# Combination and w_oa operations in halves, and row and square additions on GpSimd

## The chip, the cores and the metric

The kernel runs on one core of one Trainium2 chip. The metric is the device time of one execution in microseconds; the time of a kernel is the median of several runs. Before the change it is 2155.13 us, the median of 3 runs that lie between 2155.13 and 2161.53. The profile shows another execution, which took 2158.47 us; its span from the first to the last instruction is 2156.7 us, at a mean granted TensorE clock of 0.995.

## The reference

One layer of a decoder trunk, all in f32, over 1024 prompt tokens and 32 sample tokens that share the weights (cut to what is computed):

```python
def swiglu(x, w1, w3, w2):
    return (jax.nn.silu(x @ w1) * (x @ w3)) @ w2

def combine_groups(outs, lses):
    w = jax.nn.softmax(jnp.stack(lses, axis=-1), axis=-1)
    o = jnp.sum(jnp.stack(outs, axis=-2) * w[..., None], axis=-2)
    return o.reshape(*o.shape[:-2], ATT_OUT_W)

def trunk_layer(x, ...):
    h = layer_norm(ALPHA * x + 0.5 * swiglu(x, f1_w1, f1_w3, f1_w2), ln1_g, ln1_b)
    z = h @ w_in + b_in
    ...
    for g, (window, dil) in enumerate(ATT_GROUPS):     # 3 dilated attention groups, 4 heads each
        ...
    att = combine_groups(outs, lses)                   # 256 columns
    yb, vrows = sgu_branch(uv, sgu_ln_g, sgu_ln_b, sgu_ws, sgu_b)   # 512 columns
    mix = (jax.nn.sigmoid(ga) * (att @ w_oa) + jax.nn.sigmoid(gb) * (yb @ w_ob)) @ w_out
    h = layer_norm(ALPHA * h + mix, ln2_g, ln2_b)
    h = layer_norm(ALPHA * h + 0.5 * swiglu(h, f2_w1, f2_w3, f2_w2), ln3_g, ln3_b)
    return h, new_bufs, vrows
```

The model width is 1024, the inner width of each FFN 2816.

## The kernel before

**Tiles.** Activations lie transposed: features on the 128 partitions, tokens along the free axis. The 1056 tokens (NT; the 1024 of the prompt are NP) form 4 chunks (NC) of 264 (C). The residual stream is eight rows of 128 features (KB = 8), held for each chunk as two tiles `Y[c][j]` of 128 x (4 x 264); "rows" below means these blocks of 128 features.

**Products.** A product in f32 is made from values split in a high and a low part. `split` (L251) casts on ScalarE (ACT, L252) and subtracts on VectorE (DVE, L253); `mm3` (L237) issues three matmuls for each tile of weights, all on L241. Results gather in PSUM: three banks of tag `mm` take turns for the blocks, five of tag `ax` serve the rest. A bank is free for the next block when its eviction has read it.

**Stages.** First FFN (its large products by schemes with seven products in place of eight; its last weights, the output stage, in plain blocks), LN1, the projection w_in with attention and the gated branch beside it, then the combination of the attention groups, the products with w_ob and w_oa, w_out, LN2, the second FFN and LN3.

**The output stage of an FFN.** For each chunk c and each row n, `block(n, c)` issues 12 matmuls and the eviction L924, which adds the product to the row. Beside it run, step by step, the generators that `tick` advances from three queues (bg, slow, mid):

- `gather` (L525) adds the rows of a chunk, two by two, into a tile of 128 x 528 (L532). Its first additions are made in the last steps of the seven-product scheme, the last by `center`.
- `center` (L536) folds the two halves (L544), adds the share of the plain weights (L545), forms the mean over the features with a matmul of ones (L548) and subtracts it from the rows (L554).
- `square_step` (L572) squares a row on ScalarE (L593) and adds the squares of each pair of rows to those of the chunk (L597), 128 x 528.
- `norm` (L599) folds the squares (L603), forms the variance with three small matmuls (L606), takes the reciprocal root (L654 to L659 or L663 to L667), spreads it by matmuls (L620) and multiplies (L631).

w_out (`mix`, eviction L1707, 24 matmuls a block) uses the same helpers for LN2.

**GpSimd.** It (POOL) combines weights for the seven-product schemes (`prep`, L385 to L393) and makes small casts of one column (`held`, L109), each of which takes a buffer in its turn once the buffer is free.

**Combination and w_oa.** `combine(hp)` (L1321) works out the weights of the three groups for a pair of heads, writes them to memory (`cD`, L1354), loads them back over 64 partitions each (L1350), multiplies each group's output by them (L1361) and adds the groups (L1363). `sample_join` (L1444) does the same for the sample tokens (L1452 to L1470, with a transposition on TensorE at L1467). In `mix` (L1564) `split_att` (L1568) splits the combined outputs, `product` (L1575) multiplies a product in PSUM into a gate (L1581), `local(n)` does so for w_ob, and the loop from L1676 for w_oa: after the four chunks of row n the two gated branches are added (L1688) and the sum is split for w_out (L1690).

**The order.** Operations go to the engines in an order made before the run: a scheduler takes the program as it is written, with a model of the durations, and keeps each engine's instructions in the order it finds. What stands under `urgent` (the evictions among it) goes ahead of what is not; fences and `issue_after` fix some pairs. Each engine then works its list off in order, and an instruction that waits holds up what stands behind it.

Of the kernel before, what the change touches and what calls it, by code (L numbers as in the profile page):

```python
# [16 lines left out]
ALU = mybir.AluOpType  # L17
# [6 lines left out]
KB = D // P  # L24
NP = 1024
NS = 32
NT = NP + NS
C = 264
NC = NT // C
# [53 lines left out]
class Trunk:  # L83
# [441 lines left out]
    def gather(self, c, i, m):  # L525

        y = self.Y[c]
        new = y[i // 2][:, 2 * (i % 2) : 2 * (i % 2) + 2]
        if i == 1:
            m = self.M([P, 2, C])  # L530
        if i:
            self.nc.vector.tensor_tensor(m, y[0][:, :2] if i == 1 else m, new, op=ALU.add)  # L532
        return m

    def center(self, c, hs, rest, m=None, parts=1):
# [36 lines left out]
    def square_step(self, c, n, tail=False):  # L572

        nc = self.nc
        tt = nc.vector.tensor_tensor
        y = self.Y[c][n // KH][:, n % KH]
        if n % 2 == 0 or tail:
            self.sq = self.M([P, 2, C])
        sq = self.sq
        if tail:  # L580
            s = self.sqs[c]
            if n == KB - 2:
                with self.urgent():
                    nc.scalar.activation(sq[:, 0], y, AF.Square)
                tt(s[:, 0], s[:, 0], s[:, 1], op=ALU.add)
                tt(s[:, 0], s[:, 0], sq[:, 0], op=ALU.add)
            else:
                with self.urgent():
                    tt(sq[:, 0], y, y, op=ALU.mult)
                    tt(s[:, 0], s[:, 0], sq[:, 0], op=ALU.add)  # L590
            return
        with self.urgent():
            nc.scalar.activation(sq[:, n % 2], y, AF.Square)  # L593
        if n == 1:
            self.sqs[c] = sq
        elif n % 2:
            tt(self.sqs[c], self.sqs[c], sq, op=ALU.add)  # L597

    def norm(self, c, i, mode, Y, s):  # L599
        nc = self.nc  # L600
# [720 lines left out]
    def combine(self, hp):  # L1321
        nc = self.nc
        raw = self.raw.pop(hp)
        t = [raw[:, g] for g in range(3)]
        nat = lambda g, x: x.rearrange("p (r b) -> p b r", r=GROUPS[g][1])
        row = lambda g, x: x.rearrange("p (b r) -> p b r", r=GROUPS[g][1])
        mn = self.X([16, P], "cmin", 1)
        for g in (1, 2):
            x = mn if g == 2 else t[0][:, 0]
            nc.vector.tensor_tensor(row(g, mn), row(g, x), nat(g, t[g][:, 0]), op=ALU.min)  # L1330
        for g in range(3):
            x = nat(g, t[g][:, 0])
            nc.vector.tensor_tensor(x, row(g, mn), x, op=ALU.subtract)
        nc.scalar.activation(raw[:, :, 0], raw[:, :, 0], AF.Exp)
        nc.vector.tensor_tensor(raw[:, :, 1], raw[:, :, 1], raw[:, :, 0], op=ALU.mult)
        for g in (1, 2):
            x = mn if g == 2 else t[0][:, 1]
            nc.vector.tensor_tensor(row(g, mn), row(g, x), nat(g, t[g][:, 1]), op=ALU.add)
        nc.vector.reciprocal(mn, mn)
        for g in range(3):  # L1340
            nc.vector.tensor_tensor(row(g, t[g][:, 1]), row(g, mn), nat(g, t[g][:, 0]), op=ALU.mult)
        yield
        att = self.att[hp]
        cbs = deque()

        def load(g):
            if g < 3:
                cb = self.held([P, NP])
                for h in range(2):
                    nc.sync.dma_start(cb[64 * h : 64 * h + 64], self.cD[hp, g, h].partition_broadcast(64))  # L1350
                cbs.append(cb)

        for g in range(3):
            nc.sync.dma_start(self.cD[hp, g].rearrange("h (a x) -> (h a) x", a=8), t[g][:, 1])  # L1354
        load(0)
        load(1)
        yield from self.pause(3)
        for g in range(3):
            aT = self.attT.pop((hp, g))
            load(g + 2)  # L1360
            nc.vector.tensor_tensor(aT, aT, cbs.popleft(), op=ALU.mult)  # L1361
            if g:
                nc.vector.tensor_tensor(att[:, :NP], att[:, :NP], aT, op=ALU.add)  # L1363
            yield

    def sample_rows(self, *blocks):
# [197 lines left out]
    def mix(self):  # L1564
        nc, a = self.nc, self.a
        att, mt = [], [None] * KB

        def split_att():  # L1568
            for hp in range(2):
                h, l = self.S([P, NT], F32R), self.S([P, NT], F32R)  # L1570
                for o in (slice(0, NP), slice(NP, NT)):
                    self.split(h[:, o], l[:, o], self.att[hp][:, o])
                att.append((h, l))

# [95 lines left out]
        ta = [self.fetch_z(26 + n) for n in range(3)]  # L1670
# [4 lines left out]
        m2 = []  # L1675
        for n in range(KB):  # L1676
# [3 lines left out]
            if n + 3 < KB:  # L1680
                m = NLEAD + NTAIL - KB + n + 3
# [3 lines left out]
            for c in range(NC):  # L1685
                product(wa, att, c, ta[n])
                self.tick(0, 1)
            nc.vector.tensor_tensor(mt[n], mt[n], ta[n], op=ALU.add)  # L1688
            m2.append((self.S([P, NT], F32R), self.S([P, NT], F32R)))
            self.split(*m2[n], mt[n])  # L1690
            done += 1
            if EARLY + n < KB:
                local(EARLY + n)
# [211 lines left out]
```

## Time and profile before

| | |
|---|---|
| median of 3 runs | 2155.13 us (2155.13 to 2161.53) |
| the profiled execution | 2158.47 us |
| its span | 2156.7 us |
| instructions | 43261 |
| mean granted TensorE clock | 0.995 |
| DVE, ACT, GpSimd busy in the span | 1552.1, 889.5, 323.5 us |

How to read it: engines are PE (TensorE's matmuls), PEld (its weight loads), DVE, ACT, POOL (GpSimd) and SP (SyncE, which issues DMAs). A group of instructions stands as line, engine, operation, result <- operands, count, then busy time and the mean duration in ns; a row of the timeline as start in the span, duration, engine, line, operation, and in square brackets the idle time just before with what ended it. The names of tiles carry the pool: S, W, R, Q, M and X lie in SBUF, mm and ax in PSUM; W, R and Q hold weights, M intermediate results, X small ones. The page has the span in 40 slices of 53.9 us:

```profile
PE   9999999999999999999999999999999999999997
DVE  8876767747789834887766758787667767657887
POOL 0432322200000012223000000000323333100000
PEclk9999999999999999999999999999999999999998
```

A digit is the busy share of the slice in tenths, for PEclk the granted clock in tenths of full speed. GpSimd has work in the two FFNs' weights and in the middle of w_in, and nearly none in the stages where the rows are added and squared.

### The profile page before, as it was taken

To read this page: it belongs to the slowest core of one execution; us is meant where nothing else is said; L and a number is where in the kernel's file an instruction comes from. 1 tells how busy PE (TensorE), PEld (TensorE's weight loads), DVE (VectorE), ACT (ScalarE), POOL (GpSimd) and SP (SyncE) were. 2 spreads that over 40 slices of the span, in tenths; PEclk is the share of its full clock that TensorE was granted. 3 is DMA by queue.
4 is the path that set the end of the run, shared out by engine and by line. 5 is a ranking of instruction groups with operands and counts; after the bars stand their busy time and mean duration, and the time that the engine had idled before them with its cause. 6 is when DMAs were issued, how large, how long until landed. Compare 5 with 4: busy or idle time off the path is not lost.

```text
span 2156.7 us, 43261 instructions
## 1 busy us (share of the span) xinstructions
PE 2124.5 (99%) x17307; PEld 2086.6 (97%) x17307; DVE 1552.1 (72%) x2727; ACT 889.5 (41%) x1680; POOL 323.5 (15%) x249
## 2 busy tenths in 40 slices
PE   9999999999999999999999999999999999999997
PEld 8999999999999999999988889999999999999997
DVE  8876767747789834887766758787667767657887
ACT  5444444422124644334375544264444444421224
POOL 0432322200000012223000000000323333100000
PEclk9999999999999999999999999999999999999998
DMA  4444545598884335676865755423454544596852
GB/s 154 146 139 170 184 164 169 190 345 311 326 327 167 130 113 174 196 237 207 281 220 164 230 176 189 154 100 119 140 178 149 190 165 159 194 408 267 310 185 81
DMA packets 168378, 426.51 MB, mean 198 GB/s; under 512 B 24353, under 2 KB 59793, under 8 KB 165489
## 3 DMA queue, kind: packets, MB, share of 16 engines
q1 hardware_dynamic: 167744, 423.21, 56.4%
q8 instruction: 135, 2.21, 0.4%
q10 hardware_dynamic: 432, 0.54, 0.1%
q14 instruction: 67, 0.54, 0.1%
HBM read 304.31 MB, written 165.57 MB: 218 GB/s over the span
## 4 chain that ended last, share of the span: by engine, by line
PE 85%; DVE 5%; DMA 5%; issue 1%; POOL 1%; ACT 1%; SPq 1%; ACTq 0%; DVEq 0%; POOLq 0%
PE ax L241 44%; PE mm L241 37%; DMA M<-kv 2%; PE ax L1205 1%; DVE W L253 1%; PE ax L1252 1%; DMA R<-wz 1%; PE ax L1229 1%; DVE M L1428 1%; DMA S<-zD 1%; DMA S<-cD 1%; DVE X L1433 0%; DVE S L631 0%; DMA S<-hD 0%; PE ax L620 0%
## 5 line engine op out<-in xcount | busy, mean ns | idle before, releaser
L241 PE MATMUL mm<-S,W 128*128 128x264 f32 x5400 | 715.7, 287 | 7.9 <-ACT S L252 2.6
L241 PE MATMUL ax<-S,W 128*128 128x264 f32 x5400 | 706.7, 284 | 0.7 <-ACT S L1033 0.5
L241 PEld LDWEIGHTS mm<-S,W 128*128 128x128 f32 x5400 | 677.6, 189 | 21.6 <-issue 8.5
L241 PEld LDWEIGHTS ax<-S,W 128*128 128x128 f32 x5400 | 676.3, 188 | 3.5 <-ACT S L1033 1.7
L241 PE MATMUL ax<-S,S 128*128 128x264 f32 x3240 | 475.7, 284 | 1.8 <-ACT S L1033 1.7
L241 PEld LDWEIGHTS ax<-S,S 128*128 128x128 f32 x3240 | 427.7, 188 | 2.4 <-ACT S L1033 1.9
L241 PE MATMUL mm<-S,S 128*128 128x264 f32 x2280 | 359.6, 286 | 2.7 <-DVE S L924 2.7
L241 PEld LDWEIGHTS mm<-S,S 128*128 128x128 f32 x2280 | 311.3, 189 | 4.1 <-ACT M L593 2.2
L252 ACT CAST W<-R 128x256 fp32r<-128x256 f32 (+2 forms) x175 | 130.7, 764 | 309.3 <-PE mm L241 140.1
L385 POOL TENSOR_TENSOR Q<-R 128x512 f32<-128x512 f32 x49 | 69.9, 1428 | 797.7 <-DMA R<-w13b 219.9
L253 DVE TENSOR_TENSOR W<-R,W 128x256 fp32r<-128x256 f32 (+2 forms) x175 | 156.8, 899 | 22.4 <-ACT W L252 21.4
L252 ACT CAST W<-Q 128x1024 fp32r<-128x1024 f32 (+1 forms) x78 | 76.8, 984 | 218.6 <-POOL Q L386 88.0
L819 DVE SCALAR_TENSOR_TENSOR S<-ax,S 128x264 f32<-128x264 f32 x240 | 99.3, 427 | 66.8 <-PE ax L241 66.4
L461 DVE TENSOR_TENSOR S<-ax,M 128x264 f32<-128x264 f32 x82 | 32.6, 432 | 148.7 <-PE ax L241 148.7
L253 DVE TENSOR_TENSOR S<-Q,S 128x1024 fp32r<-128x1024 f32 (+1 forms) x78 | 111.3, 1427 | 5.5 <-ACT S L252 5.4
L109 POOL CAST S<-ones 128x1 fp32r<-128x1 f32 x36 | 13.6, 384 | 676.0 <-PE ax L241 414.0
L253 DVE TENSOR_TENSOR W<-Q,W 128x1024 fp32r<-128x1024 f32 (+1 forms) x78 | 90.3, 1158 | 29.0 <-ACT W L252 28.9
L252 ACT CAST S<-Q 128x1024 fp32r<-128x1024 f32 (+1 forms) x78 | 76.7, 984 | 67.8 <-PE ax L241 47.2
L253 DVE TENSOR_TENSOR S<-S,M 128x528 fp32r<-128x528 f32 x72 | 83.9, 1165 | 3.7 <-ACT M L252 2.4
L386 POOL TENSOR_TENSOR Q<-Q,R 128x512 f32<-128x512 f32 x49 | 82.7, 1688 | 2.7
L252 ACT CAST S<-R 128x512 fp32r<-128x512 f32 (+1 forms) x62 | 41.9, 676 | 94.2 <-DMA sumsA<-S 39.6
L393 POOL TENSOR_TENSOR Q<-R,Q 128x512 f32<-128x512 f32 x49 | 80.2, 1637 | 1.2
(209 smaller groups left out, 2051.1 us busy)
## 6 DMA issues: line engine op xcount, KB each, us to landing
ws<-st SPq DMA_DIRECT2D x144, 256.0 KB
S<-sumsA SPq DMA_DIRECT2D x63, 528.0 KB
S<-sumsB SPq DMA_DIRECT2D x63, 528.0 KB
M<-kv SPq DMA_DIRECT2D x96, 256.0 KB
sumsA<-M SPq DMA_DIRECT2D x90, 264.0 KB
sumsB<-M SPq DMA_DIRECT2D x90, 264.0 KB
R<-w13b SPq DMA_DIRECT2D x44, 512.0 KB
R<-w13a SPq DMA_DIRECT2D x42, 512.0 KB
```

What stands on the lines that cost most here:

```text
L241: mm = lambda a, b, s, e: nc.tensor.matmul(o, a[:, cc], b, start=s, stop=e, skip_group_check=True)
L252: a = self.nc.scalar.copy(hi, src)
L253: b = self.nc.vector.tensor_tensor(lo, src, hi.bitcast(F32), op=ALU.subtract)
L385: tt(s12[:, lo], cd[:, lo], cd[:, hi], op=ALU.add)
L386: tt(s12[:, hi], s12[:, lo], ab[:, lo], op=ALU.subtract)
L393: tt(s34[:, hi], ab[:, hi], s12[:, hi], op=ALU.subtract)
L461: go(one, 5, False, lambda x: tt(h[:, x, 1], one[x], p7[:, x], op=ALU.add))
L819: nc.vector.scalar_tensor_tensor(y(x, r, e), bank[x], HALF, y(x, r, e), op0=ALU.mult, op1=ALU.add)
L1205: nc.tensor.matmul(pS[h][:, r, :nk], q[e, i * P : (i + 1) * P], k[e, k0 : k0 + nk], start=True, stop=True)
L1229: nc.tensor.transpose(pT[r][:, h, o], s[:, r, h, o], self.ident)
L1252: nc.tensor.matmul(pv[0][e, (i % 4) * P : (i % 4 + 1) * P], V[:, i - (nb - 1) + b, e], sT[:, r, h, b * P : b * P + P], start=b == 0, stop= ...
L1428: nc.vector.tensor_tensor(t, t, p.unsqueeze(1).to_broadcast(t.shape), op=ALU.mult)
```

## The change

Four edits. (1) `gather`: the additions of rows 1 and 2 of a chunk's three (i = 1, 2) go to GpSimd; the last (i = 3) stays on DVE. (2) `square_step`: the additions of squares go to GpSimd, except those of the last chunk. (3) `combine`: each multiplication and addition of 128 x 1024 becomes two of 128 x 512. (4) `split_att` splits its prompt tokens in two halves of 512, and the w_oa loop adds and splits the gated branches in two halves of 528. No matmul and no DMA is added or removed.

```diff
@@ gather
         if i:
-            self.nc.vector.tensor_tensor(m, y[0][:, :2] if i == 1 else m, new, op=ALU.add)
+            engine = self.nc.gpsimd if i < KB // 2 - 1 else self.nc.vector
+            engine.tensor_tensor(m, y[0][:, :2] if i == 1 else m, new, op=ALU.add)
         return m
@@ square_step
         elif n % 2:
-            tt(self.sqs[c], self.sqs[c], sq, op=ALU.add)
+            (tt if c == NC - 1 else nc.gpsimd.tensor_tensor)(self.sqs[c], self.sqs[c], sq, op=ALU.add)
@@ combine
-            nc.vector.tensor_tensor(aT, aT, cbs.popleft(), op=ALU.mult)
-            if g:
-                nc.vector.tensor_tensor(att[:, :NP], att[:, :NP], aT, op=ALU.add)
+            cb = cbs.popleft()
+            for o in (slice(0, 512), slice(512, NP)):
+                nc.vector.tensor_tensor(aT[:, o], aT[:, o], cb[:, o], op=ALU.mult)
+            for o in (slice(0, 512), slice(512, NP)) if g else ():
+                nc.vector.tensor_tensor(att[:, o], att[:, o], aT[:, o], op=ALU.add)
             yield
@@ mix, split_att
-                for o in (slice(0, NP), slice(NP, NT)):
+                for o in (slice(0, 512), slice(512, NP), slice(NP, NT)):
                     self.split(h[:, o], l[:, o], self.att[hp][:, o])
@@ mix, w_oa loop
-            nc.vector.tensor_tensor(mt[n], mt[n], ta[n], op=ALU.add)
             m2.append((self.S([P, NT], F32R), self.S([P, NT], F32R)))
-            self.split(*m2[n], mt[n])
+            for o in (slice(0, NT // 2), slice(NT // 2, NT)):
+                nc.vector.tensor_tensor(mt[n][:, o], mt[n][:, o], ta[n][:, o], op=ALU.add)
+                self.split(*(x[:, o] for x in m2[n]), mt[n][:, o])
```

The scheduler reorders what stands around these operations. In the whole program GpSimd's list goes from 254 instructions to 305: 17 additions each come to it in the first FFN's output stage, in w_out and in the second FFN's output stage, 8 of rows and 9 of squares. In the first FFN the square additions stand behind all casts L109 of chunk 2.

DVE in the first FFN's output stage, from the eviction (L924, after the change L925) of the third block of chunk 0 to that of the fourth; L554 (L555) subtracts the mean from rows, L253 splits a weight, L532 (L533) adds rows. Before:

```order
L924 SCALAR_TENSOR_TENSOR S_5361<-mm_7973,S_5361 128x264
L554 TENSOR_TENSOR S_5361<-S_5361,ax_7971 128x528
L253 TENSOR_TENSOR S_7995<-R_7993,S_7994 128x1024
L532 TENSOR_TENSOR M_7678<-M_7678,S_5582 128x528
L554 TENSOR_TENSOR S_5361<-S_5361,ax_7971 128x528
L554 TENSOR_TENSOR S_5554<-S_5554,ax_7971 128x528 x2
L253 TENSOR_TENSOR S_8283<-R_8281,S_8282 128x1024
L924 SCALAR_TENSOR_TENSOR S_5361<-mm_8000,S_5361 128x264
```

After:

```order
L925 SCALAR_TENSOR_TENSOR S_5361<-mm_7973,S_5361 128x264
L533 TENSOR_TENSOR M_7678<-M_7678,S_5582 128x528
L555 TENSOR_TENSOR S_5361<-S_5361,ax_7971 128x528 x2
L555 TENSOR_TENSOR S_5554<-S_5554,ax_7971 128x528
L253 TENSOR_TENSOR S_7995<-R_7993,S_7994 128x1024
L555 TENSOR_TENSOR S_5554<-S_5554,ax_7971 128x528
L925 SCALAR_TENSOR_TENSOR S_5361<-mm_8000,S_5361 128x264
```

One weight split of 128 x 1024 has left this stretch, and the row addition stands ahead of the four subtractions.

DVE in the combination of the second pair of heads: L1361 (after the change L1364) multiplies by the weights loaded from `cD`, L1363 (L1366) adds the groups, L1581 (L1584) are evictions of w_ob's products, L1461 and L1464 belong to `sample_join`. The tile mm_15522 of before is mm_15532 after. Before:

```order
L1581 TENSOR_TENSOR S_15104<-S_15104,mm_15522 128x264
L1461 SCALAR_TENSOR_TENSOR X_15497<-M_15392,X_15489,X_15497 128x64
L1361 TENSOR_TENSOR S_15061<-S_15061,S_15298 128x1024
L1461 SCALAR_TENSOR_TENSOR X_15497<-M_15392,X_15489,X_15497 128x64
L1581 TENSOR_TENSOR S_15104<-S_15104,mm_15536 128x264
L1361 TENSOR_TENSOR S_14348<-S_14348,S_15302 128x1024
L1464 COPY X_15497<-X_15497 128x64
L1581 TENSOR_TENSOR S_15104<-S_15104,mm_15550 128x264
L1363 TENSOR_TENSOR S_15061<-S_15061,S_14348 128x1024
```

After:

```order
L1584 TENSOR_TENSOR S_15107<-S_15107,mm_15512 128x264
L253 TENSOR_TENSOR W_15527<-R_15526,W_15527 128x512
L1364 TENSOR_TENSOR S_15066<-S_15066,S_15303 128x512 x2
L1584 TENSOR_TENSOR S_15109<-S_15109,mm_15532 128x264
L1364 TENSOR_TENSOR S_14348<-S_14348,S_15307 128x512 x2
L1584 TENSOR_TENSOR S_15109<-S_15109,mm_15546 128x264
L1366 TENSOR_TENSOR S_15066<-S_15066,S_14348 128x512
L1584 TENSOR_TENSOR S_15109<-S_15109,mm_15560 128x264
```

The first multiplication now stands ahead of the eviction of mm_15532, and the operations of `sample_join` have gone behind; the rows between hold two halves at a time.

TensorE near the end of the program: three matmuls L606 (L607) form chunk 2's variance among the blocks of chunk 3. Before:

```order
L241 MATMUL mm_25754<-S_25072,S_25191 128x264
L606 MATMUL ax_25670<-ones,M_25513 128x1 x3
L241 MATMUL mm_25754<-S_25073,S_25191 128x264
L241 MATMUL mm_25754<-S_25072,S_25192 128x264
L241 MATMUL mm_25770<-S_24994,S_25233 128x264
```

After:

```order
L241 MATMUL mm_25808<-S_25032,S_25271 128x264
L241 MATMUL mm_25808<-S_25033,S_25271 128x264
L241 MATMUL mm_25808<-S_25032,S_25272 128x264
L607 MATMUL ax_25708<-ones,M_25551 128x1 x3
L241 MATMUL mm_25808<-S_25062,S_25271 128x264
```

The variance stood two matmuls before the end of a block; now it stands three matmuls into the next.

## Prediction

> **What bounds the kernel now.** The page first: its span, its busy shares, then the chain that ended last.
>
> ```profile
> span 2156.7 us, 43261 instructions
> PE 2124.5 (99%) x17307; PEld 2086.6 (97%) x17307; DVE 1552.1 (72%) x2727; ACT 889.5 (41%) x1680; POOL 323.5 (15%) x249
> PE 85%; DVE 5%; DMA 5%; issue 1%; POOL 1%; ACT 1%; SPq 1%; ACTq 0%; DVEq 0%; POOLq 0%
> ```
>
> TensorE is busy in all but 32 us, and the change leaves its 17,307 matmuls as they are. So an edit can only win what TensorE waits for, or lose by adding waits. Where are those waits? The view by stretches, cut at the places where the change moves instructions, tells it. Columns: us of the stretch; busy us (and instructions) of PE, weight load, DVE, ACT, POOL; granted clock; DMA share; GB/s.
>
> ```profile
> 655.00:672.00 17.00, 14.99 (x109) 14.74 (x109) 15.40 (x28) 6.94 (x12) 0.00 (x0) 0.90 0.70 236
> 672.00:700.00 28.00, 27.14 (x219) 26.66 (x218) 26.32 (x47) 16.33 (x32) 0.00 (x0) 1.00 0.28 97
> 1262.00:1303.00 41.00, 37.08 (x302) 35.79 (x303) 33.02 (x78) 16.03 (x21) 0.00 (x0) 1.00 0.55 161
> 1303.00:1357.00 54.00, 53.27 (x427) 52.05 (x425) 46.34 (x75) 21.78 (x28) 1.24 (x2) 1.00 0.60 198
> 1390.00:1452.00 62.00, 62.00 (x511) 61.81 (x510) 49.25 (x81) 32.31 (x62) 1.69 (x6) 1.00 0.20 70
> 2090.00:2120.00 30.00, 30.00 (x244) 29.74 (x243) 25.88 (x52) 10.27 (x23) 0.00 (x0) 1.00 0.00 1
> 2120.00:2145.00 25.00, 22.41 (x182) 21.93 (x181) 18.01 (x45) 12.09 (x29) 0.00 (x0) 0.99 0.22 88
> ```
>
> The output stage of the first FFN (655 to 700) loses 2.9 us, the combination (1262 to 1303) 3.9, w_oa 0.7, w_out (1390 to 1452) nothing, the second FFN's output stage nothing up to 2120, and its tail 2.6. DVE is 93% busy from 655 to 700 (41.72 of 45 us), far above its mean of 72%: there it co-bounds.
>
> **The first FFN's output stage, first wait.** TensorE's timeline:
>
> ```profile
> 660.87 3.09 PE L241 MATMUL mm<-S,S 128*128 128x264 f32 x24
> 665.97 4.70 PE L241 MATMUL mm<-S,S 128*128 128x264 f32 x24 [2.00 <-DVE S L924]
> 676.57 1.73 PE L241 MATMUL mm<-S,W 128*128 128x264 f32 x12 [0.62 <-DVE S L924]
> 680.54 4.65 PE L241 MATMUL mm<-S,S 128*128 128x264 f32 x36 [0.23 <-DVE S L924]
> ```
>
> Three banks take turns; a block of 12 matmuls lasts about 1.5 us, and the next needs the bank that L924 has still to empty. At 663.9 the fourth eviction is late by 2.00 us, and the 24 matmuls behind it take 4.70 us where the 24 before took 3.09: another 1.61. The stretches say why: one that held the wait, and the next.
>
> ```profile
> 663.25:666.67 3.42, 1.42 (x12) 1.23 (x12) 3.40 (x7) 2.32 (x5) 0.00 (x0) 1.00 0.60 216
> 666.67:670.08 3.41, 3.41 (x18) 3.41 (x17) 3.41 (x7) 1.69 (x5) 0.00 (x0) 0.50 0.79 265
> 1284.40:1287.80 3.40, 2.00 (x17) 1.81 (x16) 2.21 (x4) 0.62 (x1) 0.00 (x0) 1.00 1.05 201
> ```
>
> After a stretch with TensorE 42% busy the granted clock is 0.50 for 3.41 us; the stretch at 1284.4, 59% busy, has no such follower. I read the limit as lying between. The Trainium skill, "TensorE: Matmul & The Clock Gate", What's actually happening, gives the half-rate state after at least one idle window of about 3.4 us. The trace disagrees: 2.00 us of waiting did it. By the page the 1.61 us would not depend on this wait and would stay, and the sum would end at 2156.3.
>
> The built order drops one weight split (L253) and keeps the rest between the third and the fourth eviction:
>
> ```profile
> L253 DVE TENSOR_TENSOR S<-R,S x4: 1215/1222/1227, 656.7 to 667.4; 128x1024 fp32r<-128x1024 f32 x4
> L924 DVE SCALAR_TENSOR_TENSOR S<-mm,S x64: 399/425/434, 656.2 to 2141.5; 128x264 f32<-128x264 f32 x64
> L597 DVE TENSOR_TENSOR M<-M,M x35: 694/700/710, 668.9 to 2139.5; 128x528 f32<-128x528 f32 x35
> ```
>
> That is 1.22 us earlier; the matmul of the mean stands four matmuls later (0.5 us), and the remaining row addition, which fills that gap, covers about half of it. I take 1.0 us off the wait. Then 1.0 us stays, the stretch is 71% busy, the clock holds, and the 1.61 us go too: **-2.6 us**. Bounds: 0 (order without effect) to -3.6 (wait gone).
>
> **The same stage, later waits.** Now 0.62 + 0.23 = 0.85 us. In the new order the evictions of mm_8153 and mm_8180 have a split (1.2), two subtractions L555 (2.4 together) and L545 (0.4) between them, 4.0 us against the 2.9 us that two blocks give: a wait of 1.1. Between mm_8079 and mm_8105 stand 3.2 us: 0.3. The price of GpSimd comes on top. No row has a 128x528 addition on it; nearest is 128x512:
>
> ```profile
> L391 POOL TENSOR_TENSOR Q<-R,R 128x512 f32<-128x512 f32 x49 | 75.8, 1547 | 14.7 <-ACT M L457 11.0 <-DVE S L253 3.7
> L489 DVE TENSOR_TENSOR M<-S x18: 699/1735/1750, 78.0 to 1866.1; 128x528 f32<-128x528 f32 x18
> ```
>
> So an addition takes about 1.6 us there instead of 0.70. And it does not run beside DVE for free: L489 at 128x528, two SBUF operands, takes 1735 ns at the median in stretches where GpSimd adds, where L597 of the same shape takes 700. A DVE operation with two SBUF operands that meets a GpSimd addition pays up to 1.04 us; L924, with one operand from PSUM, keeps 399 to 434 ns throughout. Nine square additions leave DVE here (9 x 0.70 = 6.3 us), and if about half of them collide, some 4.5 us come back. The total is covered by DVE's freed time; what counts is a collision just ahead of an eviction, and I price that at 0.35. New waits 1.1 + 0.3 + 0.35 = 1.75 against 0.85: **+0.9 us**, bounds -0.85 and +6 (every collision of chunks 0 and 1 lands in front of an eviction, 6 x 1.04).
>
> **GpSimd's own queue.** It already holds the buffer casts L109, in order, and the square sums stand behind those of chunk 2. They are no hindrance as long as their buffers are free before the first sum:
>
> ```profile
> 654.07 0.42 POOL L109 CAST S<-ones 128x1 fp32r<-128x1 f32 x1 [1.28 <-PE ax L241]
> 709.21 1.12 POOL L109 CAST S<-ones 128x1 fp32r<-128x1 f32 x1 [54.73 <-PE mm L241]
> ```
>
> The last cast ahead of the sums ran at 654.07, the first sum at 668.9 (L597's first row above); the next casts come after the sums. Cost 0; without that cover chunk 0's norm would wait.
>
> **Combination in halves.** DVE and TensorE around it:
>
> ```profile
> 1284.68 1.23 DVE L1361 TENSOR_TENSOR S<-S,S 128x1024 f32<-128x1024 f32 x1 [3.20 <-DMA S<-cD]
> 1286.59 1.70 PE L241 MATMUL mm<-S,W 128*128 128x264 f32 x12 [1.40 <-DVE S L1581]
> 1287.35 1.23 DVE L1361 TENSOR_TENSOR S<-S,S 128x1024 f32<-128x1024 f32 x1 [0.91 <-DMA S<-cD]
> 1288.83 0.30 PE L1467 MATMUL ax<-ident,X 128*128 128x128 f32 x1 [0.54 <-DVE X L1464]
> 1292.91 1.74 PE L241 MATMUL mm<-S,W 128*128 128x264 f32 x12 [0.65 <-DVE S L1581]
> 1295.44 6.09 PE L241 MATMUL mm<-S,W 128*128 128x264 f32 x48 [0.79 <-DVE S L253]
> ```
>
> The multiplication waits for a DMA (3.20 us idle), not for the operation's length, and the evictions L1581 queue behind it on DVE; TensorE waits 1.40 + 0.54 + 0.65 + 0.79 = 3.38 us. Halves shorten none of the DMA. In the new order the first multiplication stands one eviction earlier relative to the blocks: mm_15532 is emptied after it, where its counterpart mm_15522 was emptied before. So TensorE runs out of banks one block (1.45 us) earlier, about 2.5 us of waiting instead of 1.40. Then 1.2 instead of 0.65, as mm_15546 waits for the second load; the 0.54 goes, since the transposition moves behind the w_ob blocks, and 0.4 is left of the last: 4.1 against 3.38, **+0.7 us**. Bounds -1.7 (half of the waits go) and +3.
>
> **w_oa in halves.** The two waits at its end:
>
> ```profile
> 1337.80 19.03 PE L241 MATMUL mm<-S,W 128*128 128x264 f32 x150 [0.46 <-DVE S L1581]
> 1356.73 0.43 DVE L1707 SCALAR_TENSOR_TENSOR S<-mm,S 128x264 f32<-128x264 f32 x1 [2.88 <-DMA S<-hD]
> ```
>
> At 1356.7 DVE waits for a load, which halves do not touch. An early half helps the first: **-0.2 us**, bounds -0.8 and +0.3 (eight extra additions and splits, on a DVE with 7.7 us to spare).
>
> **w_out and the second FFN's output.** TensorE loses nothing there now, with a DVE that is 79% and 86% busy; 17 and 17 additions leave it. **0**, bounds 0 and +3.
>
> **The tail.**
>
> ```profile
> 2143.07 0.81 PE L620 MATMUL ax<-ident,X 128*128 128x128 f32 x6 [1.66 <-DVE X L659]
> 2147.22 1.42 PE L620 MATMUL ax<-ident,X 128*128 128x128 f32 x6 [2.68 <-DVE X L667]
> ```
>
> Chunk 2's variance matmul moves five matmuls towards the end (5 x 0.12 = 0.6 us), its chain on DVE ends one small operation later (0.2), and chunk 3's variance stands behind it on TensorE: **+0.8 us**, bounds 0 and +1.3.
>
> Sum: -2.6 + 0.9 + 0.7 - 0.2 + 0.8 = -0.4 us. The profiled execution took 2158.47 us (span 2156.7 and 1.8 around it), and would take 2158.1; the median of the runs shown is 2155.13, so **2154.7 us**.
>
> **Rivals.** *Relief*: DVE, freed of additions, is never late in 655 to 700 (2.00 + 1.61 + 0.85 = 4.5 us), half of the combination's waits go (1.7) and w_oa's 0.8: 7.0 us, 2148.1. For it: each of the three waits ends on L924 behind a DVE that is 93% busy. Against: the median of 1735 ns, and a combination that waits for a DMA. *Contention* (the other side): additions on GpSimd hold up DVE's splits ahead of evictions. Price 6.2 us for chunks 0 and 1, the first gain of 2.6 gone, 0.7 and 0.8 as above, and 1 us in the second FFN: 8.7 us, 2163.8. It decides once the collisions ahead of one eviction exceed the 2.9 us lead of two banks; against it stands that six additions are spread over 20 us. The Trainium skill, "SBUF — State Buffer", Who interferes with whom, has it as a lock: of a DVE instruction with two SBUF inputs and a GpSimd one that reads SBUF, the second blocks until the first is done. The trace agrees (1735 against 700 ns). *Clock*: the 2.5 us of waiting in the combination leave a stretch under half busy; forecast plus 1.6 and 0.4, 2156.7; the 59% now are the only row for the limit.
>
> **How the numbers follow.** Forecast 0.42, clock 0.11, relief 0.25, contention 0.22: the two outer cases have a measured row each (the three waits on L924, the 1735 ns), and my forecast nets terms of one size and opposite sign. 0.3% (6.5 us, about what a measurement of this kernel can tell from no change; its runs spread from 2155.13 to 2161.53) puts forecast and clock within, 0.53; faster 0.25; slower 0.22. The likeliest's own range, from its bounds, is 2151 to 2158; over the rivals 2146.5 (relief, with the other 1.7 us of the combination gone too) to 2164 (contention's whole price).
>
> **What would show it.** Right: the wait at 664 near 1 us and a clock of 1.00 after it; the first wait in the combination above 2 us; DVE operations with two SBUF operands above 1 us beside GpSimd additions of 1.3 us or more; w_out without a wait. Wrong: a clock of 0.50 in the stretch after that wait, L597's shape on GpSimd at 0.7 us, or TensorE waiting in w_out.

## The result, and the profile after

The changed kernel takes 2162.44 us, the median of 8 runs (2160.59 to 2166.10); the kernel before took 2155.61 us beside it (8 runs, 2154.56 to 2161.53). The ratio is 1.0029, with a 95% interval of 1.0020 to 1.0038: slower by some 6 us, where 0.4 us less were forecast. A second series (11 runs beside 33 of before) gave 1.0023 (1.0014 to 1.0032). The profiled execution took 2161.17 us.

The page of the changed kernel:

```profile
span 2158.7 us, 43320 instructions
PE 2125.7 (98%) x17307; PEld 2088.3 (97%) x17307; DVE 1540.3 (71%) x2704; ACT 894.2 (41%) x1692; POOL 393.3 (18%) x300
```

GpSimd has 70 us more to do (51 additions at 1.37 us), yet DVE has only 12 us less, where 51 additions of 0.70 us, 36 us, have left it; the 28 operations that the halves add cost little (two halves of a multiplication take 1.29 us, the whole one 1.23). So about 24 us of what left DVE came back. Three of the prediction's stretches, now (columns as there):

```profile
655.00:672.00 17.00, 16.03 (x126) 15.49 (x125) 15.79 (x25) 7.26 (x12) 3.63 (x3) 1.00 0.63 208
672.00:700.00 28.00, 23.49 (x184) 22.42 (x183) 23.64 (x41) 15.98 (x31) 8.32 (x6) 1.00 0.35 125
1390.00:1452.00 62.00, 62.00 (x510) 61.80 (x510) 41.51 (x65) 30.07 (x59) 19.09 (x19) 1.00 0.21 73
```

The first stretch gained 1.04 us of busy TensorE and its clock is whole; the second lost 3.65 us, though DVE is busy for 2.7 us less in it. w_out has 19 us of GpSimd beside it and no wait.

Two profiled executions of one kernel can differ by as much as the change does, so the times of whole spans say little here. Both kernels run the same 17,307 matmuls in nearly the same order, though, and counting them tells when the same work is reached. How much later than in before that is, stretch by stretch (us; worked out from the starts of TensorE's matmuls in the traces):

| stretch, in before's time | changed kernel | its second trace | forecast |
|---|---|---|---|
| 0 to 655 | -0.6 | +0.7 | 0 |
| 655 to 720, first FFN's output | +1.8 | +1.9 | -1.7 |
| 720 to 1262, w_in and attention | -1.0 | -0.4 | 0 |
| 1262 to 1390, combination and w_oa | +1.2 | +1.5 | +0.5 |
| 1390 to 2090, w_out and second FFN | +0.5 | +0.5 | 0 |
| 2090 to the end | +0.2 | +0.2 | +0.8 |

Four stretches return within 0.3 us; their sum is 3.7 and 4.1 us. The medians of the two series lie 6.8 and 4.8 us above those of before, so 1 to 3 us of the loss have no place in this table. Where the change does nothing, the two traces differ by chance (in the first row, one window of half clock more or less at the start is the larger part). The loss sits in the two places of the second and the fourth row.

**First FFN's output.** TensorE's timeline of the changed kernel, the rows that waited:

```profile
664.06 3.19 PE L241 MATMUL mm<-S,S 128*128 128x264 f32 x24 [0.66 <-DVE S L925]
669.03 0.71 PE L549 MATMUL ax<-M,ones 128*128 128x264 f32 x2 [0.31 <-DVE M L546]
673.86 0.71 PE L549 MATMUL ax<-M,ones 128*128 128x264 f32 x2 [1.20 <-DVE M L546]
680.88 3.19 PE L241 MATMUL mm<-S,S 128*128 128x264 f32 x24 [1.25 <-DVE S L925]
694.19 5.24 PE L241 MATMUL mm<-S,S 128*128 128x264 f32 x41 [2.00 <-DVE S L925]
```

The first wait is 0.66 instead of 2.00 us and the 24 matmuls behind it take 3.19 instead of 4.70: this gain came. The later waits, 0.85 us before, are 4.76. What DVE and GpSimd did ahead of them:

```profile
664.45 3.10 POOL L598 TENSOR_TENSOR M<-M,M 128x528 f32<-128x528 f32 x2 [9.87 <-ACT M L594]
664.86 1.50 DVE L533 TENSOR_TENSOR M<-M,S 128x528 f32<-128x528 f32 x1
666.28 2.35 DVE L253 TENSOR_TENSOR S<-R,S 128x1024 fp32r<-128x1024 f32 x1
...
682.93 3.45 POOL L598 TENSOR_TENSOR M<-M,M 128x528 f32<-128x528 f32 x2 [10.20 <-ACT M L594]
683.71 1.29 DVE L667 SCALAR_TENSOR_TENSOR X<-X 128x3 f32<-128x3 f32 x1
684.93 0.42 DVE L925 SCALAR_TENSOR_TENSOR S<-mm,S 128x264 f32<-128x264 f32 x1
685.27 1.14 DVE L668 SCALAR_TENSOR_TENSOR X<-X 128x3 f32<-128x3 f32 x1
...
687.35 1.32 POOL L598 TENSOR_TENSOR M<-M,M 128x528 f32<-128x528 f32 x1 [0.96 <-ACT M L594]
688.70 0.43 DVE L604 TENSOR_TENSOR M<-M 128x264 f32<-128x264 f32 x1 [1.61 <-POOL M L598]
689.05 2.41 DVE L632 TENSOR_TENSOR S<-S,ax 128x1056 f32<-128x1056 f32 x2
691.38 2.41 DVE L555 TENSOR_TENSOR S<-S,ax 128x1056 f32<-128x1056 f32 x2
693.71 0.77 DVE L925 SCALAR_TENSOR_TENSOR S<-mm,S 128x264 f32<-128x264 f32 x2
```

Three things are to be seen. Operations with two SBUF operands that meet GpSimd's additions are long: 1.50 for 0.70, 2.35 for 1.22, and 1.29 and 1.14 us for steps on 128x3 elements that take 0.15. The eviction between them, one operand of which lies in PSUM, keeps its 0.42 us. The fold of the squares (L604) now waits 1.61 us for GpSimd. And behind the fold stand four operations of 4.7 us together, before the eviction that TensorE wants. These are three theories of the loss: **blocking**, the **wait for GpSimd**, and the **order** that the scheduler made with a freer DVE. Two of TensorE's five waits above, 0.31 and 1.20 us, are not for evictions at all: there the matmul of the mean (L549) waits for DVE's L546.

How full DVE is here, the stretches from the start of the fourth eviction L924 (L925) to that of the twentieth tell, of before and of the changed kernel (columns as in the prediction):

```profile
665.40:693.81 28.41, 26.98 (x202) 26.53 (x203) 26.96 (x49) 14.91 (x29) 0.00 (x0) 0.94 0.38 126
663.49:694.48 30.99, 25.59 (x194) 24.27 (x195) 27.99 (x45) 15.27 (x30) 9.06 (x6) 1.00 0.42 145
```

In before DVE is idle for 1.45 of 28.41 us, and for 0.4 of the first 20: DVE sets the pace here, and TensorE follows. In the changed kernel six additions have left this stretch for GpSimd, 4.2 us, yet DVE is busy for 1.0 us longer. The four collisions of the rows above bring back 4.1 us, and one weight split of 1.2 us has moved from ahead of the fourth eviction to behind it; the other DVE operations are the same. Idle time grows from 1.45 to 3.00 us, of which 1.61 are the fold's wait for GpSimd. Together the stretch is 2.6 us longer.

**Combination and w_oa**, TensorE's waits and the two stretches around the first of them:

```profile
1286.84 15.01 PE L241 MATMUL mm<-S,W 128*128 128x264 f32 x108 [2.35 <-DVE S L1584]
1315.86 16.43 PE L241 MATMUL mm<-S,W 128*128 128x264 f32 x132 [1.12 <-DVE S L1584]
```

```profile
1283.47:1286.88 3.41, 1.06 (x10) 0.85 (x8) 1.63 (x3) 0.00 (x0) 0.00 (x0) 1.00 1.01 226
1286.88:1290.30 3.42, 3.42 (x15) 3.42 (x16) 2.85 (x6) 0.42 (x1) 0.00 (x0) 0.50 1.07 260
```

The first wait in the combination is 2.35 us (1.40 before), the later ones have gone, and a window of half clock follows, in which 15 matmuls take the time of 28. That is the rival called clock. The wait at 1315.86 is new; the rows of ACT and DVE ahead of it:

```profile
1313.06 1.09 ACT L1687 ACTIVATE S<-S 128x1056 f32<-128x1056 f32 x1 [4.74 <-DMA S<-zD]
1314.05 0.60 ACT L252 CAST W<-R 128x512 fp32r<-128x512 f32 x1
1314.68 0.69 DVE L253 TENSOR_TENSOR W<-R,W 128x512 fp32r<-128x512 f32 x1 [1.64 <-ACT W L252]
1315.30 0.76 DVE L1584 TENSOR_TENSOR S<-S,mm 128x264 f32<-128x264 f32 x2
```

On ACT the gate's sigmoid, which waits 4.74 us for a load, now stands ahead of a weight's cast (in before the cast came first, at 1311.10); DVE's split waits for the cast, and two evictions stand behind the split.

### The profile page after: what moved, and what is told of

Same layout as the page of the kernel before. It is cut to its first block, busy times and chain, and to the rows that moved or that the text cites. A ratio compares the mean times of both kernels' runs of the same rounds, so it can differ in the third digit from the quotient of the medians.

```text
span 2158.7 us, 43320 instructions
## 1 busy us (share of the span) xinstructions
PE 2125.7 (98%) x17307; PEld 2088.3 (97%) x17307; DVE 1540.3 (71%) x2704; ACT 894.2 (41%) x1692; POOL 393.3 (18%) x300
## 4 chain that ended last, share of the span: by engine, by line
PE 86%; DVE 5%; DMA 5%; issue 1%; POOL 1%; ACT 1%; SPq 0%; ACTq 0%; DVEq 0%; POOLq 0%
PE ax L241 44%; PE mm L241 38%; DMA M<-kv 2%; PE ax L1206 1%; DVE W L253 1%; PE ax L1253 1%; DMA R<-wz 1%; PE ax L1230 1%; DVE M L1431 1%; DVE X L1436 1%; DVE S L632 0%; DMA S<-zD 0%; DVE S L253 0%; DMA S<-cD 0%; DMA R<-wzp 0%
## 5 line engine op out<-in xcount | busy, mean ns | idle before, releaser
L253 DVE TENSOR_TENSOR W<-R,W 128x256 fp32r<-128x256 f32 (+2 forms) x175 | 160.7, 922 | 29.2 <-ACT W L252 28.2
L253 DVE TENSOR_TENSOR S<-Q,S 128x1024 fp32r<-128x1024 f32 (+1 forms) x78 | 111.1, 1424 | 5.1 <-ACT S L252 5.1
L253 DVE TENSOR_TENSOR W<-Q,W 128x1024 fp32r<-128x1024 f32 (+1 forms) x78 | 92.0, 1180 | 28.7 <-ACT W L252 28.6
L109 POOL CAST S<-ones 128x1 fp32r<-128x1 f32 x36 | 12.7, 374 | 546.0 <-PE ax L241 216.8
L253 DVE TENSOR_TENSOR S<-S,M 128x528 fp32r<-128x528 f32 x72 | 84.5, 1174 | 2.8 <-ACT M L252 1.0
```

The lines of the kernel that those rows point to most:

```text
L253: b = self.nc.vector.tensor_tensor(lo, src, hi.bitcast(F32), op=ALU.subtract)
```

## The experiments

All start from before or from the change. The third column is the stretch 655 to 720, the fourth 1262 to 1390, each against before, from the starts of the same matmuls.

| kernel | ratio to before, 95% interval | 655-720 | 1262-1390 |
|---|---|---|---|
| x_rows | 1.0001 (0.9992 to 1.0009) | 0.0 | -0.3 |
| x_squares | 1.0016 (1.0005 to 1.0026) | +4.1 | -0.4 |
| x_combine | 0.9997 (0.9988 to 1.0005) | -0.6 | -0.3 |
| x_woa | 0.9998 (0.9989 to 1.0007) | -0.2 | +1.0 |
| x_after | 1.0023 (1.0014 to 1.0032) | +1.9 | +1.5 |
| x_port | 1.0024 (1.0015 to 1.0033) | +3.6 | +1.1 |
| x_last | 1.0013 (1.0003 to 1.0023) | +1.4 | +0.4 |
| x_split | 1.0003 (0.9993 to 1.0012) | -0.1 | +0.9 |
| x_port_short | 1.0013 (1.0003 to 1.0023) | +1.5 | +0.2 |
| x_port_copy | 1.0001 (0.9992 to 1.0010) | +0.8 | -1.2 |
| x_late_split | 0.9999 (0.9991 to 1.0008) | -2.9 | 0.0 |
| x_late_rows | 1.0006 (0.9997 to 1.0016) | -3.0 | -0.3 |

The x_port kernels do nothing new in the fourth column; its spread there, -1.2 to +1.1, is what chance does to the loads and the clock at that place, so in that column the waits count for more than the sums. The third column holds the clock too: behind the first wait there, x_combine and x_port have no window of half clock, where before has one; x_port has one behind its later wait, and x_squares has a second one at 680.6.

### The four edits one by one

x_rows is edit 1 alone, x_squares edit 2, x_combine edit 3, x_woa edit 4.

> Only the row additions go to GpSimd (edit 1). Theory A (the loss comes from the square additions: DVE's fold of the squares waits for GpSimd, 1.61 us at 687 us in the changed kernel, and what is queued behind it makes TensorE wait 2.00 us): this kernel loses nothing, -3 to +1 us against before, and TensorE's waits from 672 to 700 us stay below 1.5 us in sum. Theory B (any two-operand addition on GpSimd costs what it blocks on DVE): +1 to +3 us, with DVE operations above 1.4 us ahead of evictions. Theory C (the loss sits in the combination and w_oa): within 1 us of before.

> Only the square additions go to GpSimd (edit 2). Theory A: the first FFN's output stage is some 2 to 4 us longer than before, with L604's counterpart waiting for POOL above 1 us and a TensorE wait near 2 us behind it; the kernel is +2 to +5 us. Theory B: +2 to +4 us, spread over the three output stages, without one wait that stands out. Theory C: within 1 us of before.

> Only the combination in halves (edit 3). Theory C: TensorE's first wait in the combination goes from 1.40 to 2.4 us or more, a window of half clock may follow (1.5 us), and the kernel is +1 to +4 us. Theories A and B: within 1 us of before.

> Only the splits of the combined heads and the w_oa additions and splits in halves (edit 4). Theory C: waits of about 1.3 and 0.6 us appear at the beginning of w_oa (1314 and 1332 us in the changed kernel), +0.5 to +2 us. Theories A and B: within 1 us of before.

Only the square additions make the kernel slower by themselves. x_rows is neutral, but not for the reason that theory A had: its waits from 672 to 720 are above the 1.5 us expected. Its GpSimd additions in this stage and TensorE's waits:

```profile
647.27 2.62 POOL L533 TENSOR_TENSOR M<-M,S 128x528 f32<-128x528 f32 x2
```

```profile
664.39 3.18 PE L241 MATMUL mm<-S,S 128*128 128x264 f32 x24 [0.66 <-DVE S L925]
674.11 1.73 PE L241 MATMUL mm<-S,W 128*128 128x264 f32 x12 [1.70 <-DVE S L925]
684.05 4.04 PE L241 MATMUL mm<-S,W 128*128 128x264 f32 x31 [1.28 <-DVE S L925]
693.84 4.62 PE L241 MATMUL mm<-S,S 128*128 128x264 f32 x36 [0.44 <-DVE S L925]
```

The last addition of these ends at 650, and from 655 to 708 GpSimd does nothing here: no blocking, no wait for it. Yet the later waits are 3.42 us against 0.85. This is the **order**, but it is not a loss by itself: from the fourth eviction to the twentieth DVE does what it does in before, but for one small step, and one weight split more, which the new order took from ahead of the fourth eviction. So most of what the first wait won (0.66 for 2.00) is paid behind it. The half clock is given back in part too, as x_combine shows, which in this stage has before's order on DVE, but no half clock behind its first wait:

```profile
664.98 3.21 PE L241 MATMUL mm<-S,S 128*128 128x264 f32 x24 [1.90 <-DVE S L924]
675.17 1.73 PE L241 MATMUL mm<-S,W 128*128 128x264 f32 x12 [1.70 <-DVE S L924]
```

The 24 matmuls take 3.21 us instead of 4.70, but the next wait is 1.70 instead of 0.62: 1.1 us of the window's 1.6 come back there, because DVE reaches that eviction only 0.4 us sooner after the first wait (10.19 us instead of 10.60).

In x_squares the first wait stays at 1.90, two waits of 1.34 and 1.60 come, and a DVE operation (L544) stands idle 2.27 us until GpSimd's addition ends. Only two DVE operations collide there before 720 us, by 1.1 and 0.7 us; DVE is no busier than in before between the fourth eviction and the twentieth (26.4 us) but idle for 5.4 us instead of 1.45. So edit 2 alone loses by waits and by the second window of half clock, more than by blocking, and more (+4.1) than all four edits together (+1.8): the edits' costs do not add up.

x_combine loses nothing, against theory C: first wait 1.49 us. It is x_woa, edit 4, that has the changed kernel's 2.11 us in the combination and 1.26 at the beginning of w_oa.

### The change once more, and with the last square addition on DVE

> The change once more, on the chip of the runs beside it, for a second trace. The first trace of it was 2.2 us longer than the one of before, by stages: first FFN's output stage +1.8, combination to w_oa +1.2, w_out to the end +0.7, the rest -1.5 by chance. If the stages are the cause, this trace gives the same three figures within 0.5 us, except where a window of half clock (1.5 to 1.7 us) comes or stays away; the median is +4 to +6 us against before. If the loss lay in the attention stage (900 to 1200 us), which the change does not touch, the three figures would not return.

The three figures returned (+1.9, +1.5, +0.7; second column of the table above). The half clock in the combination came again.

```diff
-            (tt if c == NC - 1 else nc.gpsimd.tensor_tensor)(self.sqs[c], self.sqs[c], sq, op=ALU.add)
+            engine = nc.vector if c == NC - 1 or n == KB - 1 else nc.gpsimd
+            engine.tensor_tensor(self.sqs[c], self.sqs[c], sq, op=ALU.add)
```

> The change, with the last square addition of each chunk left on DVE as the last row addition is. The fold of the squares then follows an addition on DVE's own queue. Theory A: the 1.61 us idle ahead of the fold and most of the 2.00 us that TensorE waits behind it (694 us) go; 1 to 2.5 us of the change's loss come back. Theory B: one blocking addition less for each chunk, 0.5 us or less comes back.

The fold no longer waits for GpSimd, and TensorE's wait at 694 is 1.56 instead of 2.00 us: 0.4 us of the stage came back, which is theory B's figure and below A's 1 to 2.5. The median is 2.4 us below the changed kernel's beside it, but the two intervals overlap, and about 1 us of that lies in the combination and w_oa, which this edit does not touch (the wait at 1315 us is 0.51 there). The steps on 128x3 elements still take 1.30 and 1.13 us there. In the changed kernel the **wait for GpSimd** at the fold is real and small.

### Blocking alone

Before, with nothing moved; GpSimd gets 27 additions of its own, and all other engines keep their lists:

```diff
             tt(self.sqs[c], self.sqs[c], sq, op=ALU.add)
+            if c < NC - 1:
+                e = self.Y[c][n // KH][:, n % KH - 1 : n % KH + 1]
+                nc.gpsimd.tensor_tensor(e, e, self.zero.unsqueeze(1).to_broadcast([P, 2, C]), op=ALU.add)
```

> Before, with 27 additions of 128x528 added on GpSimd (rows of Y plus a zero, written back unchanged), one after each pair of squares of the chunks 0 to 2 in the three output stages. DVE, ACT and TensorE keep before's instructions in before's order, and nobody soon waits for the new additions: only the blocking of DVE's two-operand operations is added. Theory B (blocking is the loss): TensorE's waits from 670 to 720 us grow by 2 us or more, as with the square additions on GpSimd. Theory A (DVE waits for GpSimd's results and buffers, and its order changes): DVE operations of 1.4 us or more appear, but TensorE's waits there stay below 1.6 us in sum (0.85 before), and the kernel is within 1.5 us of before.

Rows of x_port: GpSimd's additions, then three DVE operations between two waits of TensorE.

```profile
L602 POOL TENSOR_TENSOR S<-S,X x27: 1061/1230/2047, 665.2 to 2137.8; 128x528 f32<-128x528 f32 x27
```

```profile
664.01 3.20 PE L241 MATMUL mm<-S,S 128*128 128x264 f32 x24 [1.90 <-DVE S L929]
665.42 2.09 DVE L253 TENSOR_TENSOR S<-R,S 128x1024 fp32r<-128x1024 f32 x1
667.43 1.29 DVE L547 TENSOR_TENSOR M<-M,S 128x264 f32<-128x264 f32 x1
671.37 1.57 DVE L599 TENSOR_TENSOR M<-M,M 128x528 f32<-128x528 f32 x1
676.81 2.45 PE L241 MATMUL mm<-S,W 128*128 128x264 f32 x12 [3.42 <-DVE S L929]
```

In before these three took 1.22, 0.42 and 0.70 us: each is longer by 0.87 us, whatever its own length. Together 2.61 us. TensorE's wait is 3.42 us where before has 0.62; but before has a window of half clock ahead of it and x_port has not, so x_combine's 1.70 is the wait to compare. From the end of the first wait to the end of this one x_combine takes 10.19 us (664.98 to 675.17) and x_port 12.80 (664.01 to 676.81): 2.61 more. Theory A, which expected waits below 1.6 us in sum, falls, and B's figure came: on a DVE that is full, a blocked operation costs TensorE all that it costs DVE. The whole kernel is as slow as the changed one without a single moved instruction. That blocking alone can cost this much is shown by it; how much of the changed kernel's loss is blocking is not.

The same with each addition cut in two of 128x264, and with plain copies in place of additions:

> The kernel with the added GpSimd additions once more, each cut in two of 128x264; DVE, ACT and TensorE keep the same order. If a DVE operation that meets an addition waits for the end of that one instruction: its excess falls from 0.87 us to half of that or less, and TensorE's wait at about 677 us (3.42 us with whole additions, 0.62 in before) falls to 1.5 to 2.5 us. If the two engines merely share the rate at which they read: the excess stays at about 0.9 us for each operation and the wait above 2.8 us.

> As the kernel with 27 added GpSimd additions of 128x528, but with plain copies (one operand) in their place, written back to the same rows; the order of the other engines stays. If an addition blocks because it holds the way to the memory while it runs, a copy that runs as long blocks as long: DVE operations that meet it are longer by nearly the copy's own duration, and TensorE's wait at 677 us is 0.62 plus some 2 to 3 of these. If the addition blocks because of its second operand, the copy blocks nothing: L253 stays at 1.22 us and the wait at 0.6 us.

The TensorE row at that place, of the short additions, then of the copies, and the split L253 beside the copies:

```profile
678.22 1.73 PE L241 MATMUL mm<-S,W 128*128 128x264 f32 x12 [2.10 <-DVE S L930]
```

```profile
677.40 1.73 PE L241 MATMUL mm<-S,W 128*128 128x264 f32 x12 [1.50 <-DVE S L929]
667.34 1.65 DVE L253 TENSOR_TENSOR S<-R,S 128x1024 fp32r<-128x1024 f32 x1
```

Short additions (0.63 us) cost up to 0.46 us an encounter, half as much, but there are more encounters: from 655 to 720 us 13 DVE operations are longer by 4.4 us in sum, in x_port 7 by 4.6. The wait is 2.10 us, in the expected 1.5 to 2.5; it stands behind a window of half clock, so it is to be compared with before's 0.62. Copies, 0.63 to 0.78 us where nothing holds them up, also cost 0.43 and give a wait of 1.50, again behind half clock: one operand blocks as well, by its duration. So an encounter costs DVE nearly the length of one GpSimd instruction, not a share of its rate, and GpSimd's instructions are held up in their turn (up to 2.05 us for 1.07 in x_port). The Trainium skill, "SBUF — State Buffer", Who interferes with whom, calls the ports that DVE and GpSimd share "an exclusive lock". These traces agree, up to 0.2 us an encounter: 0.87, 0.43 and 0.43 us are lost against instructions of 1.07, 0.63 and 0.63.

### Which half of edit 4

```diff
-                for o in (slice(0, NP), slice(NP, NT)):
+                for o in (slice(0, 512), slice(512, NP), slice(NP, NT)):
```

> Only the splits of the combined heads in halves; w_oa's additions and splits stay whole. In the order made for it the first multiplication of the combination stands one eviction earlier, as in the change. If this edit alone makes TensorE wait there: a first wait of 2.1 to 2.4 us at about 1283 us instead of 1.40, with the later ones of before (0.54, 0.65, 0.79) gone, and no wait above 0.6 us from 1310 to 1335 us, where w_oa's halves would have to be the cause. If w_oa's halves are the cause of both, this kernel is like before in both places.

```profile
1285.68 2.23 PE L241 MATMUL mm<-S,W 128*128 128x264 f32 x12 [2.05 <-DVE S L1581]
```

The split in halves alone brings the first wait of 2.05 us in the combination (2.1 to 2.4 expected), with a window of half clock behind it, and a second of 0.52; from 1310 to 1335 us there is no wait. The one at 1315 belongs to the halves of w_oa. Neither edit touches the operations that wait: both act through the order.

### Towards a version that beats both

x_late_split has none of the change but edit 3, and moves three weight splits of the next stage off the stretch:

```diff
-                if c == 2:
-                    self.early = [self.unit(self.a["wzp"][n], slot=True, ahead=AFTER) for n in range(CHUNKED)]
...
+                if mode != "out" and c == 2 and n == 3:
+                    with self.fenced():
+                        self.early = [self.unit(self.a["wzp"][m], slot=True, ahead=AFTER) for m in range(CHUNKED)]
```

> No addition on GpSimd, w_oa as before, the combination in halves, and the three weights that the next stage needs are split only after the third row of chunk 2, so that these splits (1.22 us each on DVE) no longer stand ahead of the evictions of chunks 0 and 1. If the order on DVE is what TensorE waits for in the first FFN's output stage: its wait at 664 us falls from 2.00 us to about 0.8 with no window of half clock behind it, those at 676 and 680 us go, and one of 0.5 to 1 us may come at 690; the stage is 1.5 to 3 us shorter, the kernel -1 to -4 us against before. If GpSimd's help is needed there: no gain.

```profile
663.90 3.20 PE L241 MATMUL mm<-S,S 128*128 128x264 f32 x24 [0.77 <-DVE S L924]
742.34 10.21 PE L241 MATMUL mm<-S,S 128*128 128x264 f32 x69 [2.05 <-DVE S L253]
```

The stage is 2.9 us shorter without GpSimd, with 3.9 us of DVE's time taken out of it (30.9 us busy from the first eviction to the twentieth, 34.8 in before); then TensorE, which is early, waits 2.05 us for a split of the normalised rows at 742, and the half clock behind that wait takes the rest: at 760 us the kernel stands 0.5 us behind before. x_late_rows is the same with edit 1 added and the splits after the first row of chunk 2 (`n == 1`):

> The row additions on GpSimd (edit 1) and the combination in halves (edit 3), square additions on DVE, w_oa as before, and the three weights of the next stage split only after the first row of chunk 2. The row additions of the first FFN run on GpSimd before 655 us, where no eviction waits. If what the split's delay wins (2.9 us by 690 us) was given back at 742 us because DVE was full from 690 on, this kernel, whose splits come two rows earlier, keeps 1 to 3 us of it: -1 to -4 us against before. If TensorE is bound at 742 by the chain of the norm in any order, it is given back again, within 1 us of before.

It won 3.0 us and gave them back at 741.5 us, with a wait of 2.15 us for the same split: the second of the two expectations came. Whether it is the norm's chain that binds there is not settled: from 722 to 742 us DVE is full in both kernels (19.7 and 19.5 of 20 us). No version here beats before by what can be measured.

## Why the prediction was wrong

**What bounds the kernel.** Right: TensorE's work is unchanged, and what moved are its waits and the half clock behind them; the beginning of w_oa was not among the places named. But from 665 to 685 us DVE does not co-bound, it bounds: it is idle for 0.4 of 20 us.

**First wait, -2.6 us.** Right for the wait itself, in mechanism and size; wrong in that all of it was counted as won. The wait is 0.66 us (1.0 forecast), the clock behind it 1.00, and TensorE reaches the work of 672 us 2.3 us earlier. The half clock there isn't certain in before: of eight traces with that wait of 1.9 to 2.0 us, six had it. Of the window's 1.6 us, 1.1 came back at the next wait in x_combine, and the split that had moved behind the fourth eviction had still to be done there.

**Later waits, +0.9 us.** This is the step that failed: they cost 4.0 us (from -2.8 at 672 to +1.2 at 720). It said that the collisions' total "is covered by DVE's freed time; what counts is a collision just ahead of an eviction, and I price that at 0.35". The number of collisions was about right (four, 4.1 us, against some 4.5), the cover wasn't there. An addition that leaves DVE frees 0.70 us; an encounter costs 0.8 to 1.1 (0.87 in x_port). Between the fourth eviction and the twentieth six additions left, 4.2 us, and the collisions put 4.1 us back. And on a DVE that is 93% busy and works in order, each blocked operation stands ahead of an eviction: 2.61 us on DVE were 2.61 on TensorE in x_port. The wait of 1.1 us that I read from the order between mm_8153 and mm_8180 came (1.25), in part by luck: DVE also waits 0.79 us there for a cast on ACT, which the sum did not have.

Three parts of the term were missing. The split that the order moved, 1.2 us, and part of the half clock are paid back behind the first wait, as x_rows and x_combine show without GpSimd's help. The matmul of the mean waits 1.51 us for L546, where I had looked at evictions only. And the fold waits for GpSimd, 0.4 us of the stage by x_last. They overlap, and how much of the 4.0 us on TensorE is whose in the changed kernel can't be told from these runs.

**GpSimd's queue and the casts, 0.** Right: the square additions start at 664 us, after the last cast.

**Combination, +0.7 us.** The order was read rightly: one eviction fewer ahead of the first multiplication, a first wait of 2.35 us (2.5 forecast). I put it down to the combination's halves; x_combine and x_split show that the halves of `split_att` cause it. And my limit for the clock, between 42% and 59% busy, held: the stretch was 31% busy and the next ran at 0.50, in all five traces with this order. The forecast left this to the rival clock: its window came, while the waits of 1.2 and 0.4 that I had kept behind the first did not: TensorE runs its next 108 matmuls without a wait. So part of the window's price probably came back that way, as in the first FFN.

**w_oa, -0.2 us.** Wrong: 1.12 us of a new wait, by an order on ACT that I had not looked at.

**w_out, 0.** Right: 17 additions on GpSimd, no wait. There DVE has the slack that the argument needed elsewhere. The 0.5 us between 1390 and 2090 were not followed up.

**Tail, +0.8 us.** 0.2 us: the wait at the first spread is 1.82 instead of 1.66 us.

**Rivals.** Contention was the nearest: 2163.8, with the right mechanism, and chance 0.22. Its point of decision (2.9 us of collisions ahead of one eviction) was reached in x_port's 2.6 with what was late already. I held against it that six additions are spread over 20 us; in x_port three in 7 us were enough. That its time came so near is partly luck: its 8.7 us hold 6.2 of collisions with the first gain gone, where the trace has 4.1 of collisions with the first gain made, and the table's stages sum to 4 us. The range held the time, the forecast's sign did not.

## What to carry to other kernels

Moving additions from DVE to GpSimd freed almost nothing here: beside DVE operations with two SBUF operands, each encounter costs DVE 0.8 to 1.1 us, and the addition saves it 0.70. In w_out, where DVE has time to spare, it does no harm, and there was nothing to gain. On an engine that works in order and is hardly idle, price each delay in full at whoever waits behind it, on ACT's list too. And where a scheduler sets the order, an edit's cost is read from the new order between two evictions, everywhere it differs, not from the operations that were edited; a wait that is removed by moving work behind it on the engine that sets the pace returns further on.

## What the runs showed of the hardware

The half clock comes in fixed windows. The trace's clock changes lie on a grid of 3.413 us, and whether a window is followed by half clock goes by TensorE's busy share of it. Of 14 traces, between the start and the tail, all 19 windows up to 47% busy were followed by half clock, and of those from 49% up one was (61%, in x_squares, with six matmuls of a single column in it). Two stretches of x_combine and one of x_port stand at the limit:

```profile
1210.90:1214.30 3.40, 1.59 (x19) 1.11 (x17) 3.09 (x6) 1.24 (x3) 0.00 (x0) 1.00 1.02 308
1214.30:1217.70 3.40, 3.40 (x18) 3.15 (x15) 3.40 (x7) 1.66 (x3) 0.53 (x1) 0.50 0.87 285
```

```profile
660.43:663.84 3.41, 1.68 (x14) 1.47 (x13) 3.41 (x7) 1.94 (x5) 0.00 (x0) 1.00 0.73 231
```

1.59 us busy of 3.41 was followed by 0.50, and 1.68 was not. The grid's phase differs from one execution to the next, so a wait of 2 us brings a window that does 1.6 us less work when it falls into one window, and none when it is cut in two. That is probably part of why executions of one kernel spread by 5 to 9 us; no run separates it. The Trainium skill, "TensorE: Matmul & The Clock Gate", What's actually happening, asks for an idle window of about 3.4 us; the length of the window agrees with these traces, the idleness does not: here a window that was less than about half busy was enough.
